# Score products of a decode attention: 64 query columns per batch instead of 128 columns half of zeros

## The chip, the cores and the metric

The kernel runs on one core of a Trainium2 chip. The metric is the device time of one execution, in microseconds (us). Three executions of the kernel before took 1157.09, 1162.95 and 1162.08 us; the median is 1162.08 us. TensorE (PE in the profile, PEld for its weight loads) multiplies, VectorE (DVE), ScalarE (ACT) and GpSimd (POOL) do the elementwise work, and SyncE (SP) issues nearly all the DMAs.

## The reference

One step of a hybrid decoder layer for a prompt of 512 tokens and for eight decode batches ("the sample") of 8 new tokens each, which have 2048 cached tokens. The part that matters here is the attention of the sample, with 8 heads in 2 key groups of 64 features:

```python
p_c = masked_softmax(jnp.einsum('btghd,bcgd->btghc', qg, kc), m_c)              # compressed rows
imp = jnp.einsum('btghc,cs->btgs', p_c, cover)                                  # picks 16 blocks of 64 keys
p_s = masked_softmax(jnp.einsum('btghd,btgkd->btghk', qg, sel[..., 0, :]), m_s) # selected blocks
p_w = masked_softmax(jnp.einsum('btghd,bkgd->btghk', qg, kv_win[:, :, 0]), m_w) # window of 512
o = g[..., 0:1] * o_c + g[..., 1:2] * o_s + g[..., 2:3] * o_w
```

Around it stand a gated recurrence (mixer B), the merge of both mixers, an output projection and a gated MLP. All of it is float32.

## The kernel before, in words

The program runs through stages: the recurrence and the compressed rows of the sample (to about 300 us of the span), queries, keys and values, the prompt's attention (about 430 to 562 us, method `head`, eight heads), the sample's attention (about 562 to 666 us, `sample`), the merge, and the MLP from about 700 us to the end.

The sample's batches go in four pairs. A pair has 2 batches x 64 rows (2 groups x 4 heads x 8 tokens), which stand on the 128 partitions: batch 0 of the pair on 0 to 63, batch 1 on 64 to 127. The keys of the two batches differ, so one product cannot serve both. `qpad` (line 1476) therefore hands out 128 columns for a batch, 64 of them its queries and 64 of them zeros, and the two products of a pair are added in one bank of PSUM: each adds nothing on the other batch's partitions. For this `Qs` has 128 columns for each batch, queries first and zeros behind. Four places use it: `select` (line 1494, the compressed rows, 128 keys), `score_products` (line 1554, 512 cached keys, that is four pages of each batch), and in `scores_new` line 1584 (128 new keys, bank `sm`) and line 1593 (512 window keys). The operands are float32, and the profile records each such product as two weight loads and two matmuls.

A pair needs four score groups of line 1554, called x = 0 to 3 (2 products each), then the group of line 1584 and that of line 1593. VectorE takes each out of PSUM with the mask and the row's minimum (lines 1569, 1587 and 1615, written to `sS`), ScalarE takes the exponent over 2112 columns (line 1601), VectorE scales (line 1607), TensorE transposes (line 1629), the halves are split (`pt`), and TensorE multiplies with the values (line 1637, bank `po`). The scores x = 0 to 3 of the next pair are issued between these; x = 3, the new keys and the window follow each other directly. The products of pair 0 with x = 0 and 1 are made early, during the prompt's last head (`self.early`, bank `ps_g`).

`psp` are pages split into two parts: ScalarE casts the upper part (line 330), then VectorE or GpSimd subtracts (line 331). `nsp` is the same for the window's values. The pages come through SP's queue, eight to a half, into buffers that are used in turn (`half`, line 1405; the load is line 930, tiles `pgs` and `praw`). The fourth half (`praw2`) lies where mixer B's operand `obs` was, so it can be loaded only after the last product of `branch_b` (line 1198), 16 runs of twelve matmuls that fill waits of the prompt's attention. Behind it in SP's queue come the constants `c_sample` with the masks, the window's keys (`nraw`) and the next pair's pages.

The order of instructions on each engine is chosen by a scheduler when the program is built; it works with its own model of each instruction's length. So an edit in one place can move instructions elsewhere.

Of the kernel before, what the change touches and what calls it, by code (L numbers as in the profile page):

```python
# [29 lines left out]
QKV_CUTS = (0, 262, 524, 786, 1048, 1304)  # of the columns k 0:384, v 384:512, gates 512:536, q 536:1048, v 1048:1304  # L30


# ------------------------------------------------------------------ host side: layouts and shape constants
# [60 lines left out]
def const_blob():  # L94
    """Constants side by side, grouped by the phase that loads them: the blob, and name -> (group, column, columns)."""
# [12 lines left out]
def level_masks():  # L108
    """0/1 masks of the recurrence's levels: rows s, columns in the order of the moving operand."""
# [28 lines left out]
def ktiles(w, cols):  # L138
    """[K, N] -> [N / cols, 128, K / 128, cols]: one contiguous run of a partition for each block of columns."""
    k, n = w.shape  # L140
    return np.ascontiguousarray(w.reshape(k // 128, 128, n // cols, cols).transpose(2, 1, 0, 3))


def layouts(x_prompt, x_sample, cache_cmp_kv, cache_slc_kv, page_table, state_win_kv, state_hgrn, state_ffn_conv,
# [30 lines left out]
    # compressed branch: partitions are (token parity, feature)  # L175
# [43 lines left out]
# ------------------------------------------------------------------ device side  # L219
# [57 lines left out]
class Rows:  # L277
    """Eight rows of 128 in two tiles."""
# [9 lines left out]
class Layer:  # L288
# [15 lines left out]
    # ---- small helpers  # L304
# [10 lines left out]
    @contextmanager  # L315
    def banks(self, name, **tags):
        """The phase's tiles in PSUM: tag = (banks, buffers)."""
        with self.tc.tile_pool(name=name, bufs=1, space=PSUM, reuse_waits="tile") as pool:
            self.bank_pools.update({t: (pool, n, bufs) for t, (n, bufs) in tags.items()})
            yield  # L320
# [5 lines left out]
    def split(self, hi, lo, src, scale=None, eng=None):  # L326
        """src (times scale) = hi + lo exactly, hi with the 12 bits that one pass of the tensor engine carries."""
# [13 lines left out]
    def wsplit(self, dram, kt, cols, place=None, raw=None):  # L341
        """A block of weights in its two parts: [128, part, kt, cols]."""
# [9 lines left out]
    def wcols(self, dram, cols):  # L352
        """All rows of a few hundred columns of weights, [128, part, cols] for each 128 rows."""
# [6 lines left out]
    def gemm(self, ps, parts, n0=0, n=None):  # L360
        """ps [128, 2, >=288] = sum of w.T x over parts (w split [128, 2, kt, 128], x split [128, 2, kt, 576])."""
# [11 lines left out]
    # ---- the whole program  # L373
# [73 lines left out]
    def token_sums(self, ps, sq, first):  # L447
        """ps [tokens, (block, 2)] += the sums of sq [feature, token] over the features."""
# [5 lines left out]
    def token_rms(self, p, ps, n):  # L454
        """(the mean over n features of each token's squares + eps) ** -0.5, tokens on the partitions."""
# [10 lines left out]
    def spread(self, p, rt):  # L466
        """A value for each token, tokens on the partitions -> tokens on the columns, the same for all partitions."""
# [10 lines left out]
    def prep_x(self, p):  # L478
        """x times the norm's gain, in its two parts; 1 / rms for each token, as rows and as columns."""
# [42 lines left out]
    def gemm_tok(self, ps, w, n, j):  # L522
        """ps [tokens of block j, n] = x w; the sample's block has its two parts in the two halves of the rows."""
# [11 lines left out]
    def tok_out(self, outs, ps, n, j, tmp_pool, tag="up", bufs=None):  # L535
        """outs (destination, columns, columns' end) = ps times 1 / rms."""
# [11 lines left out]
    def project(self, w, p, scale, tag="g"):  # L548
        """scale / rms * (x w), [column, token]."""
# [10 lines left out]
    # ---- mixer B  # L560
    def hgrn_consts(self):
        """Coefficients of f = fa + fb tanh(z / 2), k = fb - fb tanh(z / 2), from the softmax over the logits."""
# [18 lines left out]
    def hgrn_inputs(self, p, h, q):  # L581
        """f, k of one head [key, token]; q in its place of the moving operand."""
# [13 lines left out]
    def hgrn_values(self, p, x):  # L596
        """v of two heads by token."""
# [7 lines left out]
    def silu2(self, dst, zh, p, j=None):  # L605
        """silu(2 zh) = (tanh(zh) + 1) zh."""
# [7 lines left out]
    def totals(self, p, t4, nb, tag):  # L614
        """Products before and behind each of four parts of a block, and of all four. t4 [128, nb, 4]."""
# [16 lines left out]
    def place(self, A, pv, level, m):  # L632
        """The products of a level into their places: A [128, 2, tokens], pv [128, 2, blocks * (6 m or, with the diagonal, 10)]."""
# [10 lines left out]
    def hgrn_chain(self, p, h, f, k, mv):  # L644
# [6 lines left out]
        # level 1: parts of one token in blocks of four  # L651
# [27 lines left out]
        # the sample's eight tokens of each batch: levels 1 and 4  # L679
# [23 lines left out]
        # levels 4 and 16  # L703
# [24 lines left out]
        # level 64  # L728
# [12 lines left out]
        # k by token, the states, the outputs  # L741
# [26 lines left out]
        # the sample  # L768
# [19 lines left out]
    def readout(self, p, h, po, po2, gb):  # L788
        """RMS norm of o over the values, times silu of the gate."""
# [61 lines left out]
    # ---- compressed rows  # L851
    def cmp_weights(self, q):
# [19 lines left out]
        # the position's share, later  # L872
# [3 lines left out]
    def cmp_pos(self, q):  # L876
        """The position's share of the sums: the weights move past the position's two parts."""
# [21 lines left out]
    def cmp_gemm(self, ps, j, x, start):  # L899
        """ps += w1 of kind j times x (two parts, [128, 8, ...])."""  # L900
# [5 lines left out]
    def cmp_silu(self, p, ps, j, n, c):  # L906
        """2 silu of the rows' sums, [64, n, c] with the last of each c columns void; ps [128, n * c]."""
# [14 lines left out]
    def load_pages(self, raw, dram, lo, n):  # L922
        """n pages from entry lo of the page table, the entries loaded after the previous pages' transfers are under way."""
# [8 lines left out]
    def pages(self, q, dram, b):  # L932
        """Sixteen pages of a batch, [128, page, 128], in two parts."""
# [9 lines left out]
    def cmp_sample(self, q):  # L943
        """Compressed k [(group, feature), pair, batch, position] and v [position, pair, batch, (group, feature)].

        Each step traces a batch's products behind what TensorE has so far, and the next batch's pages."""
# [24 lines left out]
    def cmp_sums(self, q, ps, j):  # L971
        nc = self.nc
        V = nc.vector
        # 2 silu of the rows' sums, [(batch, feature), group, position]
# [932 lines left out]
```

## Time and profile before

| what | value |
|---|---|
| three executions, us | 1157.09, 1162.95, 1162.08 |
| median, us | 1162.08 |
| span of the profiled execution, us | 1156.3 |
| median less that span, us | 5.8 |
| PE busy in the span | 1111.8 us, 96% |
| DVE, ACT, POOL busy | 57%, 41%, 37% |
| data moved | 151.54 MB, 131 GB/s on average |

The span runs from the first to the last instruction of the profiled execution; what lies around it (5.8 us if that execution took the median) is outside the trace. A matmul's end is modelled and matmuls overlap, so the distance from one start to the next is what TensorE spends on one, and not the duration in the record: products of 512 float32 columns have records of 592 ns and follow each other every 0.43 us.

### The profile page before, as it was taken

To read this page: it belongs to the slowest core of one execution; us is meant where nothing else is said; L and a number is where in the kernel's file an instruction comes from. 1 tells how busy PE (TensorE), PEld (TensorE's weight loads), DVE (VectorE), ACT (ScalarE), POOL (GpSimd) and SP (SyncE) were. 2 spreads that over 40 slices of the span, in tenths; PEclk is the share of its full clock that TensorE was granted. 3 is DMA by queue.
4 is the path that set the end of the run, shared out by engine and by line. 5 is a ranking of instruction groups with operands and counts; after the bars stand their busy time and mean duration, and the time that the engine had idled before them with its cause. 6 is when DMAs were issued, how large, how long until landed. Compare 5 with 4: busy or idle time off the path is not lost.

```text
span 1156.3 us, 21362 instructions
## 1 busy us (share of the span) xinstructions
PE 1111.8 (96%) x7936; PEld 1052.7 (91%) x7936; DVE 663.1 (57%) x1182; ACT 470.9 (41%) x929; POOL 428.8 (37%) x514
## 2 busy tenths in 40 slices
PE   5999999999999899999898799999999999999998
PEld 5998899898999899989666699999999999999998
DVE  6667556664347756897778565565555556521110
ACT  5523334343454467775565454323222222211110
POOL 3663523832275545253356244323232323211010
PEclk8999899999999999999999999999999999999999
DMA  5534455454341331173688376322222222333330
GB/s 191 182 104 140 130 162 182 131 158 133 129 161 58 103 112 59 39 239 120 218 284 279 117 248 210 115 76 90 83 82 91 75 92 74 111 106 113 102 121 21
DMA packets 99273, 151.54 MB, mean 131 GB/s; under 512 B 11233, under 2 KB 66274, under 8 KB 99042
## 3 DMA queue, kind: packets, MB, share of 16 engines
q1 hardware_dynamic: 97714, 146.00, 40.2%
q0 software_dynamic: 1024, 3.54, 0.9%
q8 instruction: 62, 1.02, 0.4%
q10 hardware_dynamic: 432, 0.65, 0.2%
q14 instruction: 41, 0.34, 0.1%
HBM read 131.65 MB, written 22.62 MB: 133 GB/s over the span
## 4 chain that ended last, share of the span: by engine, by line
PE 57%; DVE 6%; DMA 2%; issue 2%; ACT 1%; SPq 1%; POOL 1%; DVEq 0%; ACTq 0%; POOLq 0%
PE ps_g L367 43%; PE ps_g L1198 2%; PE ps_hp L1305 1%; PE ps_sb L1297 1%; DVE r L1136 1%; PE ps_g L1766 1%; PE ps_g L1776 1%; PE ps_sa L1265 1%; PE ps_po L1637 1%; SPq L930 1%; POOL rr L1126 1%; PE ps_sc L1554 1%; DMA praw<-in_pkv 1%; DVE wsp L331 1%; PE ps_sa L1258 1%
## 5 line engine op out<-in xcount | busy, mean ns | idle before, releaser
L367 PE MATMUL ps_g<-h,wsp 128*128 128x288 f32 x2112 | 279.8, 294 | 0.0
L367 PEld LDWEIGHTS ps_g<-h,wsp 128*128 128x128 f32 x2112 | 279.4, 188 | 0.1
L330 ACT CAST wsp<-wraw 128x1024 fp32r<-128x1024 f32 (+3 forms) x142 | 136.4, 966 | 280.8 <-PE ps_g L367 244.5
L367 PE MATMUL ps_g<-xg,wsp 128*128 128x288 f32 x1200 | 185.8, 309 | 16.1 <-ACT wsp L330 9.7
L367 PEld LDWEIGHTS ps_g<-xg,wsp 128*128 128x128 f32 x1200 | 171.1, 197 | 23.3 <-ACT wsp L330 9.9
L331 DVE TENSOR_TENSOR wsp<-wraw,wsp 128x1024 fp32r<-128x1024 f32 (+2 forms) x93 | 114.9, 1237 | 118.9 <-ACT wsp L330 118.8
L331 POOL TENSOR_TENSOR wsp<-wraw,wsp 128x1024 fp32r<-128x1024 f32 (+3 forms) x49 | 105.9, 2161 | 171.4 <-ACT wsp L330 170.8
L367 PE MATMUL ps_g<-g,wsp 128*128 128x288 f32 x1056 | 140.9, 296 | 0.0
L367 PEld LDWEIGHTS ps_g<-g,wsp 128*128 128x128 f32 x1056 | 140.8, 189 | 0.0
L528 PE MATMUL ps_t<-wsp,xg 128*128 128x262 f32 (+1 forms) x480 | 60.9, 285 | 0.0
L528 PEld LDWEIGHTS ps_t<-wsp,xg 128*128 128x128 f32 x480 | 58.9, 189 | 0.1
L903 PE MATMUL ps_pc<-phi,w 128*128 128x256 f32 x256 | 58.6, 316 | 0.0
L330 ACT CAST phi<-praw 128x2048 fp32r<-128x2048 f32 x16 | 30.4, 1903 | 54.2 <-PE ps_pc L903 45.8
L1153 POOL TENSOR_TENSOR zg<-zg,rsb 128x576 f32<-128x576 f32 x16 | 27.4, 1712 | 67.4 <-ACT zg L1152 67.4
L1851 POOL COPY cout<-ext 128x2 f32<-128x2 f32 x22 | 4.1, 185 | 119.1 <-DVE ext L1848 119.1
L331 DVE TENSOR_TENSOR plo<-praw,phi 128x2048 fp32r<-128x2048 f32 x14 | 32.7, 2339 | 24.9 <-ACT phi L330 19.3
L903 PEld LDWEIGHTS ps_pc<-phi,w 128*128 128x128 f32 x256 | 45.7, 206 | 0.8 <-issue 0.8
L1866 DVE TENSOR_TENSOR s<-ps_g,s 128x576 f32<-128x576 f32 x22 | 16.6, 756 | 51.5 <-POOL s L1862 51.5
L1858 ACT ACTIVATE s<-cv 128x512 f32<-128x512 f32 x22 | 13.9, 632 | 78.6 <-DVE cv L1856 78.6
L903 PE MATMUL ps_pc<-plo,w 128*128 128x256 f32 x128 | 40.4, 315 | 0.0
L1847 DVE TENSOR_TENSOR ext<-ps_g,rs 128x288 f32<-128x288 f32 x22 | 10.1, 457 | 50.7 <-PE ps_g L367 50.7
L1272 ACT ACTIVATE sP<-sP,nm 128x128 f32<-128x128 f32 (+3 forms) x64 | 35.6, 558 | 8.1 <-DVE nm L1270 8.1
(428 smaller groups left out, 2003.9 us busy)
## 6 DMA issues: line engine op xcount, KB each, us to landing
wraw<-in_wFi SPq DMA_DIRECT2D x44, 512.0 KB
praw<-in_pc SPq DMA_DIRECT2D x256, 64.0 KB
praw<-in_pkv SPq DMA_DIRECT2D x80, 128.0 KB
wraw<-in_wM SPq DMA_DIRECT2D x16, 512.0 KB
wraw<-in_wFo SPq DMA_DIRECT2D x16, 512.0 KB
gbd<-zg SPq DMA_DIRECT2D x24, 288.0 KB
wraw<-in_wBr SPq DMA_DIRECT2D x24, 256.0 KB
pgs<-in_pkv SPq DMA_DIRECT2D x48, 128.0 KB
```

What stands on the lines that cost most here:

```text
L330: self.copied = nc.scalar.copy(hi, src)
L331: (eng or nc.vector).tensor_tensor(lo, src, hi.bitcast(F32), op=ALU.subtract)
L367: self.last = nc.tensor.matmul(ps[:, h, 0:HF], w[:, cw, wk, :], (x[cx] if isinstance(x, list) else x[:, cx])[:, xk, h * HF:(h + 1) * HF], ...
L528: nc.tensor.matmul(ps[:, 0:n], self.xg[cx][:, k, j * 128:j * 128 + 128], w[k][:, cw], start=(k == 0 and c == 0), stop=(k == KT - 1 and c = ...
L903: self.nc.tensor.matmul(ps, self.w1[:, cw, j, k], x[cx][:, k], start=start and k == 0 and n == 0, stop=k == 7 and n == 2, skip_group_check ...
L930: self.page_dma = nc.sync.dma_start(raw[:, i], dram[bass.ds(rv[i], 1)].rearrange("o p c -> p (o c)"))
L1126: nc.gpsimd.tensor_tensor(rr[0:r, 0:nh], ss[0:r, 0:nh], self.mhalf[0:r, 0:nh], op=ALU.pow)
L1153: nc.gpsimd.tensor_tensor(z, z, self.rsb, op=ALU.mult)
L1198: self.last = nc.tensor.matmul(ps, w[:, cw, k], self.obs[cx][:, k, c], start=n == 0, stop=n == 11)
L1272: nc.scalar.activation(s[:, b], s[:, b], AF.Exp, scale=-1.0, bias=nm[:, 1 + b, i:i + 1], accum_out=sm[:, 1 + b, i:i + 1])
L1858: nc.scalar.activation(s[:, 0:512], cv[:, 0:512], AF.Silu)
L1866: V.tensor_tensor(s.rearrange("p (a b) -> p a b", a=2), ps[:, :, 0:HF], s.rearrange("p (a b) -> p a b", a=2), op=ALU.mult)
```

## The change

`Qs` keeps 64 columns for each batch and no zeros, and `qpad` is gone. Each product takes the 64 columns of its batch and writes partitions 0 to 63 (batch 0 of the pair) or 64 to 127 (batch 1), and both start fresh instead of the second adding to the first. The number of products, the keys they read and the columns they stream stay the same. The memset of `Qs` covers half the columns. Comments and docstrings were taken out too; because `qpad` went, later lines have numbers that are 5 lower.

```diff
-        self.Qs = p.tile([128, 8, 128], F32, name="Qs")
+        self.Qs = p.tile([128, 8, 64], F32, name="Qs")
         nc.gpsimd.memset(self.Qs, 0.0)
...
-            nc.scalar.copy(self.Qs[r].rearrange("p b (x h t) -> p x h b t", x=4, h=4)[:, g],
+            nc.scalar.copy(self.Qs[r].rearrange("p b (x h t) -> p x h b t", x=2, h=4)[:, g],
...
-    def qpad(self, pr, bb):
-        at = 2 * pr * 128 + bb * 64
-        return self.Qs.rearrange("p b x -> p (b x)")[:, at:at + 128]
...
-                nc.tensor.matmul(ps[:, pr], self.qpad(pr, bb), self.kcf[:, pr, bb], start=pr == 0 and bb == 0, stop=bb == 1,
-                                 skip_group_check=True)
+                nc.tensor.matmul(ps[64 * bb:64 * bb + 64, pr], self.Qs[:, 2 * pr + bb], self.kcf[:, pr, bb], start=pr == 0,
+                                 stop=True, skip_group_check=True)
...
-            self.last = self.nc.tensor.matmul(ps.rearrange("p (n c) -> p n c", n=4), self.qpad(pr, bb),
-                                              kv[bb][:, y:y + 4, 0], start=bb == 0, stop=bb == 1)
+            self.last = self.nc.tensor.matmul(ps[64 * bb:64 * bb + 64].rearrange("p (n c) -> p n c", n=4),
+                                              self.Qs[:, 2 * pr + bb], kv[bb][:, y:y + 4, 0], start=True, stop=True)
...
-                self.last = nc.tensor.matmul(ps[:, 0:128], self.qpad(pr, bb), self.Kn.rearrange("p b t -> p (b t)"),
-                                             start=bb == 0, stop=bb == 1)
+                self.last = nc.tensor.matmul(ps[64 * bb:64 * bb + 64, 0:128], self.Qs[:, 2 * pr + bb],
+                                             self.Kn.rearrange("p b t -> p (b t)"), start=True, stop=True)
...
-            self.last = nc.tensor.matmul(ps, self.qpad(pr, bb), kw[:, bb], start=bb == 0, stop=bb == 1)
+            self.last = nc.tensor.matmul(ps[64 * bb:64 * bb + 64], self.Qs[:, 2 * pr + bb], kw[:, bb], start=True, stop=True)
```

The scheduler answers with another order from the place of `select` on. TensorE at the end of the prompt's attention, before: the last twelve products of mixer B (line 1198) stand behind the first transposes of the last head (line 1297), and the early score products stand further down (line 1554).

```order
L1305 MATMUL ps_hp<-pts,vstk 128x512
L1297 MATMUL ps_sb<-c_base,sP_6141 128x128
L1297 MATMUL ps_sb<-c_base,sP_6152 128x128
L1297 MATMUL ps_sb<-c_base,sP_6163 128x128 x2
L1198 MATMUL ps_g<-obs,wsp 128x288 x12
L1305 MATMUL ps_hp<-pts,vstk 128x512 x2
```

TensorE at the same place now: the last products of mixer B stand ahead of the second half of the head before, and the early score products (now line 1549, 64 columns) directly behind the last head's first transposes.

```order
L1198 MATMUL ps_g<-obs,wsp 128x288 x12
L1305 MATMUL ps_hp<-pts,vstk 128x256 x4
L1311 MATMUL ps_hp<-ptc,vcs 128x512 x2
L1297 MATMUL ps_sb<-c_base,sP_6133 128x128
L1297 MATMUL ps_sb<-c_base,sP_6141 128x128
L1297 MATMUL ps_sb<-c_base,sP_6152 128x128
L1297 MATMUL ps_sb<-c_base,sP_6163 128x128
L1549 MATMUL ps_g<-pgs,Qs 64x512 x4
L1305 MATMUL ps_hp<-pts,vstk 128x512
```

So two runs of line 1198 moved ahead, and behind them only the last head's own work and the score products are left. VectorE at the start of the sample's pair 0, before (`ps_sc` rows are the evictions of x = 2 and 3, `psp` the page splits):

```order
L331 TENSOR_TENSOR oas_7235<-oa,oas_7235 128x288
L331 TENSOR_TENSOR psp<-pgs,psp 128x512
L1569 ISA sS,nmp<-ps_sc,bm 128x512
L1569 ISA nmp 128x1
L331 TENSOR_TENSOR psp<-pgs,psp 128x512
L331 TENSOR_TENSOR psp<-praw_6953,psp 128x512
L1569 ISA sS,nmp<-ps_sc,bm 128x512
L1569 ISA nmp 128x1
L1587 ISA sS,nmp<-ps_sm,c_sample 128x64
```

VectorE at the same place now:

```order
L331 TENSOR_TENSOR oas_7235<-oa,oas_7235 128x288
L1564 ISA sS,nmp<-ps_sc,bm 128x512
L1564 ISA nmp 128x1
L331 TENSOR_TENSOR psp<-pgs,psp 128x512
L1564 ISA sS,nmp<-ps_sc,bm 128x512
L1564 ISA nmp 128x1
L331 TENSOR_TENSOR psp<-pgs,psp 128x512
L1582 ISA sS,nmp<-ps_sm,c_sample 128x64
```

One split fewer stands ahead of the first eviction and two fewer ahead of the new keys' eviction. ScalarE where pair 2 ends, before (`nsp` is the window's values, `praw` the next pair's pages, `pt` and `vc` what pair 2 still needs):

```order
L330 CAST nsp<-nraw 128x512 x2
L330 CAST psp<-praw_8218 128x512
L330 CAST pt<-ps_tr 128x4x64
L330 CAST psp<-praw_8244 128x512
L330 CAST psp<-praw_8218 128x512
L330 CAST pt<-ps_tr 128x8x64
L330 CAST psp<-praw_8244 128x512
L330 CAST vc<-vcf 128x2x128
```

ScalarE at the same place now:

```order
L330 CAST nsp<-nraw 128x512 x2
L330 CAST psp<-praw_8218 128x512
L330 CAST pt<-ps_tr 128x4x64
L330 CAST pt<-ps_tr 128x8x64
L330 CAST vc<-vcf 128x2x128
L330 CAST psp<-praw_8244 128x512
L330 CAST psp<-praw_8218 128x512
```

Three casts of the next pair's pages moved behind `pt` and `vc`; GpSimd's subtractions of these pages wait for their casts.

## Rows read from the trace of the kernel before

**Rows 1.** The page's 40 slices of the span: TensorE's busy tenths.

```profile
PE   5999999999999899999898799999999999999998
```

**Rows 2.** Busy time by stretch (us), count, granted clock, DMA share, GB/s.

```profile
604.00:628.00 24.00, 21.82 (x126) 16.10 (x126) 18.90 (x41) 14.17 (x30) 13.51 (x13) 1.00 0.85 272
628.00:652.00 24.00, 19.63 (x96) 13.68 (x95) 17.49 (x33) 11.73 (x24) 8.73 (x8) 0.93 0.38 124
```

**Rows 3.** TensorE's groups by shape: count, busy us, mean ns, idle before.

```profile
L1554 PE MATMUL ps_sc<-praw,Qs 128*128 128x512 f32 x40 | 19.8, 624 | 0.0
L1593 PE MATMUL ps_sc<-nraw,Qs 128*128 128x512 f32 x16 | 7.6, 597 | 1.0 <-DMA nraw<-in_wk 1.0
L1554 PE MATMUL ps_sc<-pgs,Qs 128*128 128x512 f32 x16 | 7.6, 595 | 0.0
L1554 PE MATMUL ps_g<-pgs,Qs 128*128 128x512 f32 x8 | 3.6, 592 | 0.0
L1584 PE MATMUL ps_sm<-Kn,Qs 128*128 128x128 f32 x16 | 2.4, 274 | 0.0
```

**Rows 4.** Timeline of TensorE: start us, length us, line, tiles, count.

```profile
617.70 0.61 PE L1584 MATMUL ps_sm<-Kn,Qs 128*128 128x128 f32 x4
618.14 1.88 PE L1593 MATMUL ps_sc<-nraw,Qs 128*128 128x512 f32 x4
```

**Rows 5.** Timeline of TensorE around products with 64 weight columns, mixer B.

```profile
188.71 0.56 PE L367 MATMUL ps_g<-xg,wsp 128*128 128x288 f32 x3
189.20 0.68 PE L734 MATMUL ps_ps<-Q,K 128*64 128x64 f32 x8
189.81 0.43 PE L716 MATMUL ps_lv<-mvl,K 128*128 128x192 f32 x1
...
77.50 0.53 PE L367 MATMUL ps_g<-xg,wsp 128*128 128x288 f32 x2
```

**Rows 6.** Chain of waits, 548 to 578 us: start, length, what.

```profile
549.63 0.47 PE ps_hp L1305 x4
...
551.34 1.60 PE ps_g L1198 x12
...
554.28 1.59 PE ps_g L1198 x12
...
556.29 0.34 SPq L930
...
560.74 5.74 DMA c_sample<-in_consts
...
568.73 1.75 DVE psp L331
571.48 2.16 ACT sS L1601 x2
```

**Rows 7.** Waits of SP's queue, 545 to 665 us: total us, times, longest.

```profile
SPq L930 <- PE ps_hp L1305: 3.4, 1, 3.4
```

**Rows 8.** Timeline of VectorE, then GpSimd, from 630.9 us.

```profile
630.70 0.69 DVE L331 TENSOR_TENSOR psp<-pgs,psp 128x512 fp32r<-128x512 f32 x1
631.30 5.34 DVE L331 TENSOR_TENSOR nsp<-nraw,nsp 128x512 fp32r<-128x512 f32 x2
...
631.76 1.29 POOL L331 TENSOR_TENSOR psp<-pgs,psp 128x512 fp32r<-128x512 f32 x1
633.00 2.48 POOL L331 TENSOR_TENSOR psp<-praw,psp 128x512 fp32r<-128x512 f32 x2
```

**Rows 9.** Timeline of TensorE at group x = 2 of pairs 1, 2, 3.

```profile
589.62 1.88 PE L1554 MATMUL ps_sc<-pgs,Qs 128*128 128x512 f32 x4
...
613.37 1.88 PE L1554 MATMUL ps_sc<-praw,Qs 128*128 128x512 f32 x4
...
637.03 0.50 PE L1637 MATMUL ps_po<-vc,pt 128*128 128x256 f32 x2 [2.84 <-DVE pt L331]
...
641.02 2.84 PE L1554 MATMUL ps_sc<-praw,Qs 128*128 128x512 f32 x4
```

## The prediction, made blind

> **What bounds the kernel now.** I read the 40 slices first: TensorE is at nine tenths nearly throughout and falls to 7 and 8 only around the sample's attention [rows 1]. The windows there show why: from 604 to 628 us TensorE is busy for 21.8 of 24 us while the DMA engines are busy for 0.85 of the time at 272 GB/s, and from 628 to 652 us it falls to 19.6 us and they to 0.38 [rows 2]. So two pacers stand close together: TensorE, and the stream of pages. A saving on TensorE counts in full only where the stream has run out, which is the last pair.
>
> The changed products are 80 records of 512 columns and 16 of 128 in that stage (40 + 16 + 8 of line 1554, 16 of line 1593, 16 of line 1584) [rows 3]; the 16 records of `select` are small and left at nothing, hidden in the fully busy prompt stage. From the timeline: the group of line 1593 starts at 618.14 and its four records of 1.88 us end with one of 0.59, so the starts are 0.43 us apart; the 128-column group takes 618.14 - 617.70 = 0.44 us, 0.11 for each [rows 4]. A group of 512 columns therefore costs 4 x 0.43 = 1.72 us, all of them together 80 x 0.43 + 16 x 0.11 = 36 us.
>
> **What the change does to a group.** The number of records and streamed columns stays, so nothing is saved unless products on different halves of the array run at the same time. Call the records A1, A2 (batch 0) and B1, B2 (batch 1). No row of before shows two halves at work: its products with 64 weight columns all use the same half. Bounds: nothing overlaps, four slots, 1.72 us; everything overlaps, two slots, 0.86 us. I take three slots, 1.29 us: A2 needs the half that A1 holds, and if records start in program order only A2 and B1 can run together, then B2.
>
> The Trainium skill, TensorE: Matmul & The Clock Gate, Part 3 (Packing small matmuls), says that matmuls on different column groups run concurrently and that matmuls start and end in program order. No run here shows the first half yet. By it a group takes the three slots that I took.
>
> There is a price that the rows do show. Eight products with 64 weight columns start at 189.20; the three before them are 0.13 us apart, so they would have started at 188.71 + 3 x 0.13 = 189.11. Their 0.68 us less a last record of 0.22 leaves 0.46 for seven steps of 0.058 (0.41): 0.05 more, since the first weights were not loaded ahead. The next full-width product starts at 189.81 instead of 189.20 + 0.05 + 8 x 0.058 = 189.71, and after such a return the second start comes 0.53 - 0.29 = 0.24 us after the first and not 0.13 [rows 5]. In: 0.09 + 0.05. Out: 0.10 + 0.11. A visit to the 64-column form costs 0.35 us, each time that the queue goes there and back. A single group then takes 1.29 + 0.35 = 1.64 against 1.72: 0.08 saved. The run x = 3, new keys, window is one visit: 1.72 + 0.44 + 1.72 = 3.88 us becomes six slots of 0.43 and one of 0.11 (each group's first record runs beside the last of the group before): 2.69 + 0.35 = 3.04, 0.84 saved.
>
> On the path of a pair lie x = 2 and this run, between the products with the window's values and the transposes; x = 0 and 1 lie ahead of a wait of TensorE for VectorE. So each of pairs 1 to 3 gains 0.08 + 0.84 = 0.9 us on the path. For pair 3 it counts in full; for pairs 1 and 2 I take a bit over half, as the page stream runs at 0.85: **-2.0 us** in all (bounds: with two slots, 3 x 2.5 = -7.5; with four, 3 x 0.7 = +2.1).
>
> **What the order does.** The chain before the sample: the last products of line 1198 from 554.28, then SP's page load at 556.29, the queue down to `c_sample` (issued 560.74, 5.74 us to land), a page split on VectorE to 568.73 + 1.75 = 570.48, the evictions, and the exponent at 571.48 [rows 6]. SP had waited 3.4 us for TensorE there [rows 7]. Now the last twelve of line 1198 stand ahead of work that came before them: the second half of the head before with the first transposes, 551.34 - 549.63 = 1.71 us, and pieces of the last head, 554.28 - (551.34 + 1.60) = 1.34 us [rows 6], 3.1 us together, so the stream can start up to 3.1 us earlier, and VectorE evicts x = 3 and the new keys before two splits, one of which took 1.75 us. I take **-2.6 us** for the exponent of pair 0 (bounds 0 and -3.4). What that costs: the two fillers no longer cover the last head's splits (ScalarE's cast, then VectorE's subtraction, 0.69 us for this shape [rows 8]; I take the cast as nearly as long), and only the early products stand between. One exposed split of half its length: **+0.7 us** (bounds 0 and 2.6, two whole ones).
>
> **A stall that may go.** VectorE's first `nsp` split starts at 631.30, and the two together take 5.34 us where one of this shape takes 0.69; GpSimd runs three page splits back to back to 635.48 in that time [rows 8]. The values of pair 2 come late, TensorE waits 2.84 us, and then the group x = 2 takes 2.84 us instead of 1.88 at the lower clock; the step from pair 2 to 3 is 641.02 - 613.37 = 27.65 us where that from 1 to 2 was 23.75 [rows 9]. This costs 3.9 + 0.96 = 4.9 us. In the new order ScalarE casts only one of the next pair's pages before `pt` and `vc`, so GpSimd cannot run its splits in one piece. I take **-3.0 us** (bounds 0, if VectorE is held as long, and -4.9).
>
> Sum: -2.0 - 2.6 + 0.7 - 3.0 = **-6.9 us**. The span of 1156.3 becomes 1149.4; with the 5.8 us around it, 1155.2 us, against the median 1162.08. (One of the three runs took 1157.09, so the reference itself is uncertain by some us.) From the merge on, the orders agree but for a few products; I cost it at nothing, since TensorE is full there.
>
> **The rivals.**
> *The halves run one after the other.* For it: no row shows them together. Then each visit only costs: x = 2 and the run, 2 x 0.35 x 3 = +2.1 on the path in place of -2.0: 1162.08 + 2.1 - 2.6 + 0.7 - 3.0 = 1159.3 us. Chance 0.22.
> *The stream paces and the stall stays.* The products overlap, but pages come when they came, and VectorE is held as before: only pair 3's 0.9 and part of the head count, -0.9 - 1.5 + 0.7 = -1.7, 1160.4 us. For it: the DMA share of 0.85 [rows 2]; against it: SP's one long wait was for TensorE [rows 7]. Chance 0.20.
> *VectorE is held in other pairs.* The same mechanism as the stall: GpSimd's splits in one piece when `nsp` or `pt` is due, in two of pairs 0 to 3. It costs 4.9 us each; one repeat leaves the sum where it was without the -3.0, and from the second on the kernel is slower: -2.0 - 2.6 + 0.7 + 2 x 4.9 - 4.9 = +1.0, and with a third +5.9, 1163 to 1168 us. For it: every engine's order in all pairs has changed, and it hit one of four pairs before. Chance 0.12.
> *The products don't take the form of two halves.* If they ran full width as before, only the order would act: -2.6 + 0.7 - 3.0 = -4.9, 1157.2 us. The 64-row forms in the new order speak against it. Chance 0.04.
>
> **How the numbers follow.** The forecast has 0.42, with its own range 1150 to 1159. The range 1148 to 1165 adds the rivals and the upper bound of the stall's return; below it lie only the two-slot bound and all gains together. This kernel's time can be told from no change by about 0.5%, 5.8 us, so faster means below 1156.3 and slower above 1167.9. Faster: 0.65 of the forecast's share, a third of the full-width case, a few hundredths of each of two others, 0.27 + 0.02 + 0.04 + 0.04, and for gains above my values by the two-slot bound 0.05: 0.42. Slower: 0.4 of the third rival's share, and 0.05 for serial halves that also lose the head's gain: 0.10. The rest, 0.48.
>
> **What would show it.** Overlap: in a group of 512 columns the start of batch 1's first record stands a few ns behind that of batch 0's second, and the group's successor starts about 1.6 us after it; 0.43 between all four means serial. The visits: weight loads that start only with their matmul at each change of form. The head: SP's wait of 3.4 us gone and the exponent near 569 us. The stall: steps of about 23 us between groups x = 2 of pairs 1, 2 and 3, and no `nsp` split above 2 us. I am wrong if the sample's attention (562 to 666 us) does not shrink, or if the prompt stage loses more than 2 us to waits for `pts`.

## The result and the profile after

The changed kernel took 1146.18 us (median of four executions, 1145.21 to 1148.71) against 1161.42 us: ratio 0.9895, 95% interval 0.9865 to 0.9925. A second comparison, with executions of both kernels side by side, gave 1146.78 against 1157.96 us, ratio 0.9918 (0.9892 to 0.9944). So it is faster by about 1%. The direction was forecast; the time lies 1.8 us below the low end of the range, since the gain was larger than forecast.

The stretches of the profile of after, with the columns of [rows 2]:

```profile
604.00:628.00 24.00, 21.30 (x134) 14.94 (x133) 17.79 (x44) 14.25 (x29) 13.91 (x14) 1.00 0.95 301
628.00:652.00 24.00, 18.88 (x125) 14.09 (x123) 15.38 (x35) 13.75 (x28) 9.32 (x9) 1.00 0.54 172
```

The DMA share rose from 0.85 to 0.95 and more records pass in the same time. The sample is about 11 us shorter now, so a stretch does not hold the same work as before; the second one now holds the end of the pairs. TensorE's groups by shape in the profile after; the form is 128*64 instead of 128*128 [rows 3]:

```profile
L1549 PE MATMUL ps_sc<-praw,Qs 128*64 128x512 f32 x40 | 13.2, 613 | 0.1
L1549 PE MATMUL ps_sc<-pgs,Qs 128*64 128x512 f32 x16 | 4.3, 618 | 0.0
L1588 PE MATMUL ps_sc<-nraw,Qs 128*64 128x512 f32 x16 | 4.3, 608 | 1.2 <-DVE nmp L1564 0.7 <-DMA nraw<-in_wk 0.6
L1549 PE MATMUL ps_g<-pgs,Qs 128*64 128x512 f32 x8 | 1.9, 605 | 0.0
```

One record takes about as long as before, but the busy time of the same number of records fell from 19.8 + 7.6 + 7.6 + 3.6 = 38.6 us to 23.7: in most groups the halves work at the same time. The timeline of TensorE at the scores of pair 1 of after, group x = 2, then x = 3, new keys and window, shows how:

```profile
585.87 1.08 PE L1549 MATMUL ps_sc<-pgs,Qs 128*64 128x512 f32 x4
586.88 1.10 PE L1723 MATMUL ps_tr<-c_sample,t 128*128 128x64 f32 x8
587.91 1.08 PE L1549 MATMUL ps_sc<-pgs,Qs 128*64 128x512 f32 x4
588.82 0.39 PE L1579 MATMUL ps_sm<-Kn,Qs 128*64 128x128 f32 x4
589.04 1.03 PE L1588 MATMUL ps_sc<-nraw,Qs 128*64 128x512 f32 x4
590.20 1.04 PE L1331 MATMUL ps_sm<-oas,wsp 128*128 128x288 f32 x6
```

Four records whose last is 0.59 us long end after 1.08 us, so the last starts 0.49 us after the first, not 1.29. The four starts in the trace are 585.867, 585.874, 586.347 and 586.354: the two batches start 0.007 us apart, twice. From the group's start to the start of the transposes it is 586.88 - 585.87 = 1.01 us where it was 615.09 - 613.37 = 1.72 [rows 9], and from x = 3 to the product behind the window 590.20 - 587.91 = 2.29 (0.13 of it a wait) where it was 619.46 - 615.93 = 3.53 at the scores of pair 2 in the trace of before:

```profile
615.09 1.00 PE L1728 MATMUL ps_tr<-c_sample,t 128*128 128x64 f32 x8
615.93 1.94 PE L1554 MATMUL ps_sc<-praw,Qs 128*128 128x512 f32 x4
...
619.46 2.15 PE L1331 MATMUL ps_sm<-oas,wsp 128*128 128x288 f32 x12
```

The starts of the group x = 2 in pairs 2 and 3 of after (pair 1 is the first row above) [rows 9]:

```profile
605.42 2.01 PE L1549 MATMUL ps_sc<-praw,Qs 128*64 128x512 f32 x4
...
628.20 2.25 PE L1549 MATMUL ps_sc<-praw,Qs 128*64 128x512 f32 x4
```

These two groups take 2.01 and 2.25 us and not 1.08: here the halves ran one after the other. In pair 2 the four records start at 605.42, 605.90, 606.36 and 606.84, because the weight load of batch 1 waited for its pages while the half of batch 0 worked:

```profile
605.42 0.19 PEld L1549 LDWEIGHTS ps_sc<-praw,Qs 128*64 128x64 f32 x2
606.36 0.19 PEld L1549 LDWEIGHTS ps_sc<-praw,Qs 128*64 128x64 f32 x2 [0.75 <-DMA praw<-in_pkv]
```

The group x = 2 of pair 3 and the group x = 3 of pair 2 also start batch 1 late; what it waited for there, the profile does not name. In these three groups the last record starts 1.42, 1.65 and 1.02 us after the first, against 0.49 where both halves have their operands: together 2.6 us that the halves did not give (an estimate from these starts).

The exponents of the four pairs on ScalarE:

```profile
568.63 2.06 ACT L1596 ACTIVATE sS<-sS,nm 128x2112 f32<-128x2112 f32 x1 [0.34 <-DVE nm L1595]
...
590.16 2.06 ACT L1596 ACTIVATE sS<-sS,nm 128x2112 f32<-128x2112 f32 x1 [1.39 <-DVE nm L1595]
...
611.84 2.06 ACT L1596 ACTIVATE sS<-sS,nm 128x2112 f32<-128x2112 f32 x1 [0.94 <-DVE nm L1595]
...
635.76 2.07 ACT L1596 ACTIVATE sS<-sS,nm 128x2112 f32<-128x2112 f32 x1 [2.57 <-DVE nm L1595]
```

The steps between exponents are 21.53, 21.68 and 23.92 us; before they were 23.75, 23.76 and 28.60. SP's waits for TensorE in the stretch of [rows 7], after:

```profile
SPq L930 <- PE ps_hp L1305: 1.8, 1, 1.8
SPq L930 <- PE ps_g L1198: 1.6, 1, 1.6
```

They still add to 3.4 us, and yet the exponent of pair 0 comes earlier. That was the first sign that a step of the prediction had the wrong cause.

### Where the time went, by stage

All kernels below are compared by the same four points: the first product of `select`, the last product of the prompt's heads (line 1311), the exponent of pair 0, and the first product of the merge. "Prompt" is the first to the second, "head" the second to the third, "sample" the second to the fourth. The wait is TensorE's for `pt` on VectorE from 555 to 672 us, nsp the longest split of the window's values. V order is that of VectorE, ScalarE and GpSimd in the sample, P order that of TensorE and SP and of the other engines in the prompt. The ratio is the time against the kernel before; the stages come from one profiled execution of each kernel.

| kernel | products | P order | V order | prompt | head | sample | wait for pt | longest nsp | ratio (95%) |
|---|---|---|---|---|---|---|---|---|---|
| before | 128 | old | old | 101.84 | 8.98 | 103.97 | 11.6 | 4.74 | |
| e6, before again | 128 | old | old | 101.71 | 8.96 | 104.88 | 12.4 | 5.53 | one execution |
| e9 | 128 | old | new | 101.82 | 6.68 | 97.35 | 6.1 | 2.26 | 0.9935 (0.9912 to 0.9957) |
| e1 | 128 | new | new | 104.23 | 6.71 | 95.89 | 5.1 | 2.17 | 0.9935 (0.9910 to 0.9960) |
| e2 | 64 | old | old | 99.74 | 8.97 | 107.17 | 16.9 | 4.70 | 0.9954 (0.9927 to 0.9982) |
| e10 | 64 | new | old | 103.21 | 8.96 | 108.03 | 16.5 | 4.75 | 1.0027 (1.0005 to 1.0049) |
| after | 64 | new | new | 103.25 | 6.69 | 92.32 | 5.4 | 1.76 | 0.9895 (0.9865 to 0.9925) |
| e5, after again | 64 | new | new | 103.33 | 6.69 | 93.57 | 5.9 | 1.77 | 0.9918 (0.9892 to 0.9944) |
| b2 | 64 | old | new | 99.99 | 6.68 | 96.02 | 5.7 | 0.68 | 0.9891 (0.9858 to 0.9924) |

Prompt and sample together are 205.8 and 206.6 us before and 195.6 and 196.9 after: 10 us less. These sums of prompt and sample tell the three parts of the change apart. The V order is worth most: 206.9 (e2) to 196.0 (b2) with the halves, 205.8 to 199.2 (e9) without. The halves are worth 3 to 4.5 us with the new V order (199.2 to 196.0, 200.1 to 195.6 or 196.9) and nothing with the old one (205.8 or 206.6 to 206.9). The P order is worth nothing that these sums show with the new V order (199.2 and 200.1 without the halves, 196.0 against 195.6 and 196.9 with them), and with the old one the halves are 4.3 us longer for it (206.9 to 211.2, e10). Two profiles of one kernel differ by 0.8 and 1.3 us in these sums, so the small steps are rough.

What lies ahead of `select` is the same work in all, and yet its end lies anywhere from 455.4 to 461.1 us in these profiles; it was 2.0 us earlier in the first profile of after. That is scatter, not the change, and the kernel before scatters in full executions too (1150.74 to 1165.31 us in 25 of them). So of the 15.2 us between the medians of the first comparison (11.2 in the second) the stages explain 10. The merge took 65.5 us to the MLP where it had taken 64.6 (64.9 and 64.3 in the second profiles). It is longer in all nine profiles with changed products or a changed TensorE order (64.9 to 66.7) than in the five with neither (64.3 to 64.6), so the change seems to cost up to 1 us there; why is open.

### The profile page after: what moved, and what is told of

It reads as the page before. It is cut to its first block, busy times and chain, and to the rows that moved or that the text cites. A ratio compares the mean times of both kernels' runs of the same rounds, so it can differ in the third digit from the quotient of the medians.

```text
span 1145.1 us, 21336 instructions
## 1 busy us (share of the span) xinstructions
PE 1100.3 (96%) x7936; PEld 1043.7 (91%) x7936; DVE 659.3 (58%) x1182; ACT 471.2 (41%) x929; POOL 430.1 (38%) x514
## 3 DMA queue, kind: packets, MB, share of 16 engines
q8 instruction: 62, 1.02, 0.4%
## 4 chain that ended last, share of the span: by engine, by line
PE 76%; SPq 6%; DMA 5%; DVE 5%; issue 3%; POOL 3%; ACT 2%; POOLq 0%; DVEq 0%; ACTq 0%
PE ps_g L367 51%; SPq L930 5%; PE ps_t L528 3%; PE ps_pc L903 2%; PE ps_g L1198 2%; PE ps_lv L367 2%; PE ps_hp L1305 2%; PE ps_sb L1297 2%; DMA praw<-in_pkv 1%; PE ps_sa L1265 1%; PE ps_g L1761 1%; DMA wraw<-in_wF 1%; PE ps_g L1771 1%; PE ps_ps L528 1%; DMA wraw<-in_wM 1%
## 5 line engine op out<-in xcount | busy, mean ns | idle before, releaser
L367 PEld LDWEIGHTS ps_g<-xg,wsp 128*128 128x128 f32 x1200 | 172.6, 198 | 23.7 <-ACT wsp L330 10.3
L331 POOL TENSOR_TENSOR wsp<-wraw,wsp 128x1024 fp32r<-128x1024 f32 (+3 forms) x49 | 108.6, 2216 | 186.3 <-ACT wsp L330 183.1
L903 PE MATMUL ps_pc<-phi,w 128*128 128x256 f32 x256 | 56.3, 307 | 0.0
L331 DVE TENSOR_TENSOR plo<-praw,phi 128x2048 fp32r<-128x2048 f32 x14 | 32.7, 2338 | 23.7 <-ACT phi L330 23.5
L903 PEld LDWEIGHTS ps_pc<-phi,w 128*128 128x128 f32 x256 | 43.3, 194 | 0.8 <-issue 0.8
```

The source lines that it names most:

```text
L331: (eng or nc.vector).tensor_tensor(lo, src, hi.bitcast(F32), op=ALU.subtract)
L367: self.last = nc.tensor.matmul(ps[:, h, 0:HF], w[:, cw, wk, :], (x[cx] if isinstance(x, list) else x[:, cx])[:, xk, h * HF:(h + 1) * HF], ...
L903: self.nc.tensor.matmul(ps, self.w1[:, cw, j, k], x[cx][:, k], start=start and k == 0 and n == 0, stop=k == 7 and n == 2, skip_group_check ...
```

## The experiments

For the orders, the built programs of both kernels were read; they trace the same instructions in the same sequence, so one's order can be put on the other by queueing each instruction behind the one ahead of it in a table.

**e1 and e2: products and order crossed.** e1 is the kernel before with the line below and the changed kernel's table for every engine; e2 the changed kernel with the table of before.

```diff
-        Layer(tc, a, o, tap if taps is not None else None).run()
+        Layer(tc, a, o, tap if taps is not None else None).run(); in_order(tc, nc)
```

> Products with 128 columns as before, every engine's order as in the changed kernel. Theory (order and overlap both pay): the new order brings the head of the sample forward by about 2 us and takes away the 4.7 us VectorE stall of pair 2, the prompt loses about 1.4 us; so about 1155 to 1156 us, the steps between the groups x = 2 about 23.5 us each. Rival A (all is overlap of the halves): 1160 to 1162 us, steps as before. Rival B (all is order): 1146 to 1148 us, steps 21.5 us as in the changed kernel.

> Products with 64 columns in two halves, every engine's order as before the change. Theory: pairs of records start within 0.01 us of each other, each pair of batches is about 2.2 us shorter, the 4.7 us nsp split of pair 2 stays; about 1153 us. Rival A (overlap alone makes the gain): 1146 to 1148 us. Rival C (the page stream paces the pairs, the order makes the gain): 1159 to 1162 us.

Measured 1153.69 and 1154.67 us against 1161.53. By the times each part gives about half. The profiles say more: with the new order the sample is 95.89 us even with the old products; with the old order it is 107.17 us even with the halves, and TensorE waits 16.9 us for `pt`, more than the 11.6 before. What the halves save there is waited away again, and the clock fell: from 566 to 652 us the mean granted clock is 0.88 in e2 and 0.98 in before and in after. e2's own gain in time is only partly explained: its prompt is 2.1 us shorter, and its profiled execution reached `select` 3 us earlier than the mean of the others in the table, which is scatter; prompt and sample together are 206.9 us, no shorter than before. What remains of it is open.

**e3: ScalarE's casts later in pair 2.** My theory was that the place of ScalarE's casts let GpSimd subtract pages without a pause. ScalarE's order there:

```diff
 L330 CAST pt<-ps_tr 128x4x64
-L330 CAST psp<-praw_8244 128x512
-L330 CAST psp<-praw_8218 128x512
 L330 CAST pt<-ps_tr 128x8x64
-L330 CAST psp<-praw_8244 128x512
 L330 CAST vc<-vcf 128x2x128
+L330 CAST psp<-praw_8244 128x512
+L330 CAST psp<-praw_8218 128x512
+L330 CAST psp<-praw_8244 128x512
```

> The kernel before with three ScalarE casts of the next pair's pages moved behind pt and vc at the end of pair 2, nothing else. Theory (VectorE's nsp split is held while GpSimd subtracts pages without a pause): both nsp splits there take at most 1.9 us, the step between the groups x = 2 of pairs 2 and 3 falls from 27.65 to about 23.8 us, the time by about 4 us to 1157 us. Rival (the split is held by something else, such as the stream's writes): nsp stays above 4 us, the time at 1160 to 1162 us.

Measured 1159.91 us, ratio 0.9989 (0.9961 to 1.0017), sample 108.52 us, waits for `pt` 13.6 us. The stall had left pair 2 and stood in pair 1, with a split of 5.81 us. A miss. (That the edit moved it is not shown: e6 below has a stall in pair 1 without any edit.)

**e6 and e7: is the stall an accident, and do the casts decide it?** e6 is the kernel before, unedited; e7 makes e3's edit in pairs 0, 1 and 2.

> The kernel before once more, one profile. Theory (the stall belongs to the order, the pair that it hits varies): one nsp split of 4 us or more in pair 1 or 2, sample 104 to 109 us, exponent of pair 0 at 9.0 us behind the prompt's end. Rival (the stall was an accident of the first profile): no nsp split above 2.2 us, sample about 99 us.

> The kernel before with ScalarE's three casts of the next pair's pages behind pt and vc in pairs 0, 1 and 2, nothing else. Theory (GpSimd's run of page splits without a pause holds VectorE's nsp split, and the casts' place makes that run): no nsp split above 2.2 us in any pair, steps between exponents of 24 to 25 us, sample 99 to 101 us, time 4 to 6 us below the kernel before. Rival (the place of the casts doesn't decide it, GpSimd's own wait for zm does): a split above 4 us is still there in one pair, sample 104 us or more, time as before.

e6 had two such splits, in pairs 1 and 2; here VectorE, then GpSimd in pair 1 of e6:

```profile
604.25 4.96 DVE L331 TENSOR_TENSOR nsp<-nraw,nsp 128x512 fp32r<-128x512 f32 x2
609.13 0.41 DVE L331 TENSOR_TENSOR pt<-ps_tr,pt 128x256 fp32r<-128x256 f32 x1
```

```profile
604.16 0.73 POOL L1323 DMA_DIRECT2D zm<-gbd  x1 [0.63 <-DMA gbd<-zm]
604.92 3.73 POOL L331 TENSOR_TENSOR psp<-praw,psp 128x512 fp32r<-128x512 f32 x3
```

GpSimd's three splits end at 608.65, and the two `nsp` splits that VectorE does in 1.28 us in pair 2 of after end at 609.21. The same holds for pair 2 before [rows 8] and for pair 1 of e2 and e3: each long split ends 0.56 us behind such a run. So VectorE is held while GpSimd subtracts. The Trainium skill, SBUF — State Buffer, section "🎯 Summary: rules for kernel authors", says that of a VectorE operation with two inputs in SBUF and a GpSimd operation that reads SBUF the second to issue blocks until the first finishes. These traces agree that one of the two is held, but not on which: by the profile's starts, which are rough on GpSimd, VectorE's split is the first (604.85 against 604.92 us in e6, 631.30 against 631.76 before), and it is held over three operations in a row (4.35 us in e6 for a split that takes 0.68).

But e7 fell the other way: no split above 3.08 us, and yet the sample is 111.55 us and the time 1165.13 us, ratio 1.0067 (1.0043 to 1.0091). VectorE at the end of pair 2 of e7:

```profile
641.79 0.41 DVE L331 TENSOR_TENSOR pt<-ps_tr,pt 128x256 fp32r<-128x256 f32 x1
644.27 1.34 DVE L331 TENSOR_TENSOR psp<-praw,psp 128x512 fp32r<-128x512 f32 x1 [2.07 <-ACT psp L330]
645.54 0.68 DVE L331 TENSOR_TENSOR pt<-ps_tr,pt 128x512 fp32r<-128x512 f32 x1
```

A page split of the next pair stands between the two `pt` splits in VectorE's queue. Since its cast is later now, VectorE waits 2.07 us for it, and `pt`, which TensorE needs at once, waits behind it. TensorE waited 17.1 us for `pt` in all. The later casts shortened what held `nsp`, but the wait came back in VectorE's queue, so the place of the casts alone does not decide it.

**e9 and e10: the order of VectorE, ScalarE and GpSimd.** e9 is the kernel before with the changed kernel's order of VectorE, ScalarE and GpSimd in the sample alone; e10 the reverse on the changed kernel. The edit is the table; what it does on VectorE at the end of pair 0 (e9):

```diff
 L331 TENSOR_TENSOR nsp<-nraw,nsp 128x512 x2
 L331 TENSOR_TENSOR pt<-ps_tr,pt 128x4x64
-L331 TENSOR_TENSOR psp<-pgs,psp 128x512
 L331 TENSOR_TENSOR pt<-ps_tr,pt 128x8x64
```

> The kernel before, with VectorE's, ScalarE's and GpSimd's order in the sample's stage as in the changed kernel; TensorE's and SP's order as before. Theory (page splits of the next pair stand ahead of the last pt and of nsp on VectorE, and wait for their pages and casts; it needs VectorE's order, ScalarE's alone does not do): TensorE's waits for pt fall from 11 to about 5 us, no nsp split above 2.2 us, exponent of pair 0 up to 1 us earlier, sample 97 to 99 us, 1152 to 1155 us. Rival (TensorE's and SP's order make the gain): waits for pt 10 us or more, sample 104 us or more, time as before.

> The changed kernel, with VectorE's, ScalarE's and GpSimd's order in the sample's stage as before; TensorE's and SP's order and the halves as changed. Theory: waits for pt back at 10 us or more, a nsp split above 4 us in pair 1 or 2, sample 100 to 105 us, 1153 to 1158 us: the halves gain little while these waits decide. Rival (the halves and TensorE's order make the gain): sample 92 to 95 us, 1145 to 1149 us.

Both went the theory's way, and further than its ranges. e9: 1151.38 us against 1157.66, sample 97.35 us, with TensorE's and SP's order untouched. e10: 1160.59 us, sample 108.03 us, slower than the kernel before although it has the halves. Three engines' queues change together here. GpSimd's changes too: behind its load of `zm` at 631.00 us the kernel before has three page splits in one piece [rows 8], and in the new order the first of them stands ahead of that load (e9 has two splits ahead of the load at 628.31 and one behind it before GpSimd waits). What VectorE's queue and what GpSimd's contributes was not tested apart. In e10 the clock fell as well: from 566 to 652 us the mean granted clock is 0.84, so part of that stretch ran at 1.2 GHz, the lower of the two levels, against 0.98 in after, which differs in the V order alone, and 1.00 in e9. First e10, then e9:

```profile
566.00:652.00 86.00, 65.28 (x372) 46.27 (x371) 59.28 (x128) 45.80 (x92) 45.29 (x43) 0.84 0.72 229
```

```profile
566.00:652.00 86.00, 77.56 (x452) 58.37 (x452) 66.92 (x150) 50.12 (x99) 46.07 (x47) 1.00 0.76 242
```

In e10 a group at the lower level follows two waits for `pt`, of 1.14 and 1.22 us; its records start 0.91 us apart instead of 0.48:

```profile
590.84 1.20 PE L1632 MATMUL ps_po<-nsp,pt 128*128 128x256 f32 x8 [1.22 <-DVE pt L331]
591.97 1.97 PE L1549 MATMUL ps_sc<-pgs,Qs 128*64 128x512 f32 x4
```

e9 also brought the exponent of pair 0 from 8.98 to 6.68 us behind the prompt's end, more than the 1 us that I allowed, and e10 put it back to 8.96. VectorE at the start of the sample in e9:

```profile
563.07 0.68 DVE L1569 CUSTOM_DVE_ANT_1 sS<-ps_sc,bm 128x512 f32<-128x512 f32 x1
563.68 0.08 DVE L1569 DVE_READ_ACCUMULATOR2_ANT nmp<- 128x1 f32 x1
563.74 1.35 DVE L331 TENSOR_TENSOR psp<-pgs,psp 128x512 fp32r<-128x512 f32 x1
565.01 0.68 DVE L1569 CUSTOM_DVE_ANT_1 sS<-ps_sc,bm 128x512 f32<-128x512 f32 x1
565.62 0.07 DVE L1569 DVE_READ_ACCUMULATOR2_ANT nmp<- 128x1 f32 x1
565.62 1.15 DVE L331 TENSOR_TENSOR psp<-pgs,psp 128x512 fp32r<-128x512 f32 x1
566.68 0.21 DVE L1587 CUSTOM_DVE_ANT_0 sS<-ps_sm,c_sample 128x64 f32<-128x64 f32 x1
```

The first eviction stands ahead of both page splits, and that of the new keys follows the second; before, it stood behind a third split of 1.75 us and another eviction [rows 6].

**e4 and e8: does the page stream pace the pairs now?** e4 moves the merge's eight weight loads to GpSimd's queue, e8 moves two merge runs, one each from pairs 0 and 1, to pair 3.

```diff
-MWQ = "sync"
+MWQ = "gpsimd"
...
-PLAN = {"A0": 2, "A1": 2, "A2": 2, "A3": 2}
+PLAN = {"A0": 1, "A1": 1, "A2": 2, "A3": 4}
```

> The changed kernel with the merge's weight loads (line 338 called from merge_half, 8 of 256 KB) on GpSimd's queue instead of SP's. Theory (SP's queue now paces the pairs: pages at 0.52 us each and waits of these loads for their buffers stand ahead of pages): steps between the groups x = 2 of 1 us less, sample 2 to 4 us shorter, 1142 to 1144 us. Rival (the DMA engines themselves are full at 0.90 to 0.95): no change, 1145 to 1147 us. Rival (GpSimd's queue holds its splits up behind these loads): 1148 us or more.

> The changed kernel with one merge product run instead of two in the waits of pairs 0 and 1 and four instead of two in pair 3 (PLAN), so 0.25 MB of weights and 0.3 MB of gates less pass the queue in each of these pairs. Theory (the stream of pages paces pairs 0 to 2 now): steps between exponents from 21.5 to about 20 us, pair 3 longer by at most two runs of 1.6 us, 1143 to 1146 us. Rival (TensorE paces the pairs): steps fall by the run's 1.6 us and pair 3 grows by as much, no change. Rival (pair 3 has no waits to fill): 1147 to 1150 us.

e4: 1149.10 us, ratio 0.9902 (0.9875 to 0.9929), sample 91.46 us, so no change that can be told from the kernel after; the 2 to 4 us of the theory did not come. e8: 1161.78 us, outside all three ranges, sample 106.92 us, with waits for `pt` of 13.0 us and 27.17 us from the last exponent to the merge instead of 18.5. The scheduler answered e8 with other orders on all engines, so it doesn't settle the stream. Perhaps TensorE's merge runs fill waits in pairs 0 and 1 that nothing else fills; this run does not show it.

**e5, b1 and b2: the kernel after again, and two tries at a better one.** b1 moves two of VectorE's instructions in the prompt; b2 takes the halves with V order new and P order old.

```diff
-L331 TENSOR_TENSOR obs<-obr,obs 128x576 x3
-L331 TENSOR_TENSOR wsp<-wraw,wsp 128x512
+L331 TENSOR_TENSOR obs<-obr,obs 128x576 x2
 L1246 TENSOR_TENSOR sc<-ps_sa,c_prompt 128x128
 L1316 TENSOR_TENSOR oa<-ps_hp,pup 64x512
+L331 TENSOR_TENSOR obs<-obr,obs 128x576
+L331 TENSOR_TENSOR wsp<-wraw,wsp 128x512
```

> The changed kernel once more, for the spread of its stages and for its time beside the kernels of this job. Theory: what lies ahead of select varies by some us from execution to execution and is not the change; from select to the end of the prompt 103.2 us, the exponent of pair 0 at 6.7 us behind that, the sample 91 to 93 us, 1145 to 1149 us in all. Rival (the short sample of the first profile was a lucky execution): the sample 95 us or more, a nsp split of over 4 us.

> The changed kernel, with VectorE's line 1246 and line 1316 of one prompt head moved ahead of the third obs split and of a weight split. Theory (the 1.9 us wait of TensorE at line 1305 is queueing on VectorE): the wait goes, select to the end of the prompt 101.4 us instead of 103.3, 1144 to 1146 us. Rival (the obs split that comes later now holds a product of mixer B up, or the wait moves to the last heads): 103 us, no change.

> The changed products; TensorE's and SP's order as before the change, VectorE's, ScalarE's and GpSimd's order in the sample's stage as in the changed kernel, in the prompt as before. Theory (the halves save about 3 us in the sample and 2 us up to the prompt's end once VectorE's order is right; TensorE's and SP's new order gives nothing and costs 2.4 us in the prompt): select to the end of the prompt 99.7 us, exponent of pair 0 at 6.7 us behind it, sample 93 to 95 us, 1143.5 to 1146 us. Rival (the halves need TensorE's new order too): sample 97 us or more, 1148 to 1151 us.

b1 aimed at this wait in the prompt of after, TensorE first, then VectorE:

```profile
490.94 0.47 PE L1305 MATMUL ps_hp<-pts,vstk 128*128 128x512 f32 x1 [1.94 <-DVE oa L1316]
```

```profile
486.07 3.32 DVE L331 TENSOR_TENSOR obs<-obr,obs 128x576 fp32r<-128x576 f32 x3 [0.51 <-PE ps_g L367]
489.32 0.68 DVE L331 TENSOR_TENSOR wsp<-wraw,wsp 128x512 fp32r<-128x512 f32 x1
489.92 0.28 DVE L1246 TENSOR_TENSOR sc<-ps_sa,c_prompt 128x128 f32<-128x128 f32 x1
490.12 0.67 DVE L1316 TENSOR_TENSOR oa<-ps_hp,pup 64x512 f32<-64x512 f32 x1
```

Its prompt is 101.64 us instead of 103.3, nearly as expected; in the time (1147.56 us, ratio 0.9899, 0.9871 to 0.9927) 1.7 us don't show. b2's prompt is 99.99 us, nearly as expected, and its sample 96.02 us, 1 us over the theory's range, with 3.8 us in one wait for the window's keys:

```profile
PE ps_sc L1588 <- DMA nraw<-in_wk: 3.8, 1, 3.8
```

1146.32 us, ratio 0.9891 (0.9858 to 0.9924). Neither is told apart from the kernel after.

## Why the prediction was right in direction, and which steps failed

**"I take three slots": too cautious by one.** The step was that records start in program order, so that only A2 and B1 run together. Measured: A1 with B1, A2 with B2, two slots, wherever both batches have their operands. Each half takes its own records in order, and the halves don't wait for each other. At the scores x = 3 and new keys of pair 2 of after, where batch 1 starts 0.57 us late, this is seen directly:

```profile
609.09 1.19 PE L1549 MATMUL ps_sc<-praw,Qs 128*64 128x512 f32 x3
610.00 0.38 PE L1579 MATMUL ps_sm<-Kn,Qs 128*64 128x128 f32 x2
610.12 0.59 PE L1549 MATMUL ps_sc<-praw,Qs 128*64 128x512 f32 x1
610.55 0.38 PE L1579 MATMUL ps_sm<-Kn,Qs 128*64 128x128 f32 x2
```

The two records of line 1579 for batch 0 start at 610.00 and 610.11 us, before the last of line 1549 at 610.12, which stands ahead of them in the program; at 0.27 us against 0.59 they also end first. The Trainium skill, TensorE: Matmul & The Clock Gate, Part 3 (The mechanism), has matmuls start and end strictly in program order; on different column halves this trace shows otherwise, and the measurement decides. That they run together it has right. Taken by their first records, the four products still start in program order; it is later records and ends that pass each other. The price of a visit was nearly right: 0.21 us from the product before to the first record (0.12 without a switch), 0.05 more to the second, and 586.88 - (586.35 + 0.43) = 0.10 out, with 0.05 more behind it (0.11 forecast). The term was -2.0; with the new order on both sides (e1 against after) the halves are worth 200.1 less 195.6 or 196.9, -3.2 to -4.5 us over prompt and sample, 0.9 to 1.0 of it in the prompt, where I had set them at nothing. In the sample that is 2.3 to 3.6 us. Pair 1 shows 0.71 + 1.24 = 1.95 us of gain with all halves together, which would be about 5.9 us in three pairs (an estimate); the groups that ran one after the other took about 2.6 of it back. My bound for two slots, 3 x 2.5, was itself too wide: it takes off the price of one visit in each pair where the rest of the working takes two, with which it is 3 x (2.80 - 0.70) = 6.3.

**"The exponent of pair 0, -2.6": the size held, the cause didn't.** The exponent came 2.3 us earlier against the prompt's end. I had derived it from the last run of line 1198 and SP's load behind it. SP waited 3.4 us all the same, and e9 gives the whole 2.3 us with TensorE's and SP's order of before. The V order did it, and VectorE's rows show the way: evictions ahead of page splits, which I had named only in passing. That the size held was luck. The chain had put down 5.74 us to the landing of `c_sample` [rows 6], but what came after it stood in VectorE's queue.

**"One exposed split, +0.7": +1.5 us, elsewhere.** The prompt grew from 101.8 to 103.3 us; by e1 the order costs 2.4 us there, and the halves give 1.0 back. The last head's waits for `pts` are 0.7 us in three; the rest is the wait for line 1316 that b1 removed, in the middle of the prompt, where I had expected no change.

**"The stall goes, -3.0": it went, and the sample's order gave more.** e9 against before: head and stall together are 205.8 - 199.2 = -6.6 us (-7.4 against e6), where I had -2.6 - 3.0. The place failed: I had read ScalarE's queue, and with its casts alone moved a stall was still there (e3) or the time grew (e7). The orders of VectorE, ScalarE and GpSimd together decide it: the longest `nsp` split is 3.08 to 5.81 us in all six profiles of the old V order, e3 and e7 included, and at most 2.26 us in the seven of the new one (2.92 in e8, whose orders are its own). That a split of the next pair's page should not stand ahead of `pt` in VectorE's queue is seen in e7; how much of the rest is VectorE's queue and how much GpSimd's shorter runs is open. The rival "VectorE is held in other pairs" is not what the changed kernel did, but stalls in pair 1 of e3, e6 and e10 show that it was a real danger.

**The rival "the stream paces and the stall stays"** fell as a whole, since the stall went and the steps between exponents shrank. But its first half holds in part. With V order new, TensorE's waits for pages and window keys in the sample are 1.3 us in e9 and 0.6 in after (2.1 in e5, 4.5 in b2), but these leave out a half that waits while the other works: the 2.6 us of the three groups above, and 3.1 us by the same working in e5. So the stream still takes part of what the halves could give. **"The halves run one after the other"** fell with the timeline, except in those groups.

**The sum's base.** I added 5.8 us around the span. Where span and time belong to one execution (1145.1 and 1146.86 us, 1153.6 and 1155.59 us) it is 1.8 and 2.0. The profiled execution of before therefore took about 1158.3 us (an estimate from these), some 3.8 less than the median from which I counted, and from it the sum reads 1151.4. The measured time lies 9.0 us below my 1155.2: 3.8 of it is this base, that is scatter of the kernel before, 3.3 a gain over prompt and sample that I had too small (6.9 against 10.2), and the remaining 1.9 lies outside these stages, where the profile of after reached `select` 2.0 us earlier.

## What to carry to other kernels

Products that use half the weight columns cost half only when two of them, on different halves, are issued together and both have their operands (three groups here had not); then a pair takes the time of one, and what is left to watch is the switch of form, 0.14 us in and 0.15 out. Before counting such a gain on the path, read the queue of the engine that feeds the next product: while VectorE is late with `pt`, what TensorE saves it waits (e2). And an edit that makes a scheduler reorder is two changes: cross products and order before believing either.

## What was not expected of the hardware

The two column halves of TensorE take their records independently, even past each other: 610.11 us for a record of a later product, 610.12 for one ahead of it in the program. VectorE's subtraction of two SBUF operands stands still for as long as GpSimd runs three or four subtractions back to back, 4.35 to 5.81 us instead of 0.68, although by the profile's starts it came first.
